# A transformer stack: compressed scores of the second token tile amid the first heads, the experts' choice ahead of the second tile's parts of X

## The chip, the cores and the metric

The kernel runs on one core of a Trainium2 chip. A core has TensorE (PE: matmuls, results in PSUM), VectorE (DVE), ScalarE (ACT), GpSimd (POOL) and SyncE (SP), each with its own queue, worked off in order; they wait for one another by semaphores. Transfers between HBM and on-chip memory are issued by SP and ACT. The metric is the device time of one execution in microseconds (us), as the median of several runs. TensorE's clock has two levels, 2.4 and 1.2 GHz; the profile gives the granted share (1.00 or 0.50).

## The reference: what is computed

256 tokens of 1024 numbers pass two blocks, and then a third of another kind, all in float32. Block one is windowed attention and a feed-forward. Block two, around which the change lies, is attention with three branches (compressed, selected and windowed keys) and a mixture of 8 experts, of which each token takes the best two:

```
s_c = einsum('bqkgd,bckd->bkgqc', qc, kcc) * scale          # compressed scores, 15 keys
p_c = _masked_softmax(s_c, cmp_end[None, :] <= tpos[:, None])
...
o = g[..., 0:1] * o_c + g[..., 1:2] * o_s + g[..., 2:3] * o_w
...
x = _layer_norm(DN_ALPHA * x + h, ln_gain[i, 0], ln_bias[i, 0])
...
logits = (xt @ router).astype(jnp.float32)
vals, ids = lax.top_k(logits, TOP_K)
w = jax.nn.softmax(vals, axis=-1)
gate = jnp.sum(jax.nn.one_hot(ids, N_EXPERTS) * w[..., None], axis=1)
for e in range(N_EXPERTS):
    out = out + gate[:, e:e + 1] * _swiglu(xt, w_gate[e], w_up[e], w_down[e])
```

Block three reads a memory of 256 further tokens, whose keys and values depend on no earlier block.

## The kernel before

Tokens stand in two tiles of 128 (`tt` 0 and 1). Each float32 weight tile is split into a high part (`wh`, a cast on ScalarE, L253 or L256) and a low part (`wl`, a subtraction on VectorE, L254 or L257), and a product is three matmuls (high by high, low by high, high by low: L274 to L276, and L1173 to L1175 in the experts). SP loads weights into a ring of raw tiles some tiles ahead. The order on each engine is set by a scheduler from the order in which the code is written, from priorities and from where pools of on-chip memory overlap: a pool that lies over another's place comes after it in that order.

The attention of block two (`nsa`) projects queries, keys and values, turns the queries of each tile (`rope64` on VectorE, transposes at L470, copies `qh`, `ql` at L474 and L475), and then computes compressed scores of both tiles, one after the other (L868 the mask, L872 24 matmuls of 32 columns a tile, L874 to L888 the softmax), in the two PSUM buffers of the pool `at`. Then come the heads, by `cc` and `tt`, in two halves each: scores in the four PSUM buffers of the pool `mm` (L909, mask L911), maximum (L913), exponentials on ScalarE (L917), transposes (L928), products with the values (L934 to L936) in an `at` buffer `ops`. Between the parts of the heads `fill` emits runs of the memory's keys and values of block three, L1900, which use `mm` as well and end with a copy `mkv` (L1903) and a store.

`route_load`, called when the heads are through in the code, loads the router's tables on ScalarE's queue (`rt` L964, `first` L976, `slots` L978, `uf` L981) into a pool `route`, and makes from them `gb` (the router times the norm's gain), `sums`, `c` (L973, L974) and `ub`.

`heads_out` multiplies by the output weights; `ln_part` adds and takes statistics, and for a tile that is complete calls `ln_rows`: transposes of the row that is not yet normed (L417, copied into `xT` at L418), mean and root (L382, L349, a power on POOL), and X in parts, `Xh` and `Xl`, by two passes on VectorE over 1024 columns, a cast on ScalarE and a subtraction (L424 to L428). These parts are what the experts gather their tokens from.

`moe` begins with the choice. Logits are the router's product with `xT` (L1002, 8 matmuls a tile, each two passes), corrected by mean and root (L1006 to L1008). Comparisons among the 8 logits, ties by `first`, give `sel` and `selb` (L1014 to L1022). Five small matmuls count places (L1025 to L1029), and `pos`, `cnt` and the one-hot tiles `oh` follow (L1031 to L1060). A branch on the count (L1131, L1132) comes before the first gather, matmuls of `oh` with `Xh` and `Xl` (L1106), and the experts' products.

Of the kernel before, what the change touches and what calls it, by code (L numbers as in the profile page):

```python
# [8 lines left out]
F32 = mybir.dt.float32  # L9
F32R = mybir.dt.float32r  # L10
BF16 = mybir.dt.bfloat16
AF = mybir.ActivationFunctionType
OP = mybir.AluOpType
# [3 lines left out]
P = 128  # L17
# [7 lines left out]
def f(ap):  # L25
    return ap.bitcast(F32)
# [72 lines left out]
class Net:  # L99
# [305 lines left out]
    def ln_rows(self, tt):  # L405


        nc, y = self.nc, self.y[tt]
        if not self.ln_xT:
            self.xT = self.xp.tile([P, KD, T], F32, tag="xh", name="xT")  # L410
            self.Xl = self.xp.tile([P, 2, D], F32R, tag="xl", name="Xl")
            self.Xh, self.lns, self.ln_xT = [], [], True
        hs = [slice(h * 512, h * 512 + 512) for h in range(2)]
        for h in range(2):
            tp = self.tr.tile([P, 4, P], F32, tag="tr", name="tr")
            for k in range(4):
                nc.tensor.transpose(tp[:, k], y[:, h * 512 + k * P:h * 512 + (k + 1) * P], self.idn)  # L417
            nc.scalar.copy(self.xT[:, h * 4:h * 4 + 4, tt * P:(tt + 1) * P], tp)  # L418
        mu, rs = self.ln_stats(tt)
        self.lns.append((mu, rs))  # L420
        Xh = self.xp.tile([P, D], F32R, tag=f"X{tt}", name="Xh")
        self.Xh.append(Xh)
        for s in hs:
            nc.vector.scalar_tensor_tensor(y[:, s], y[:, s], mu, self.lng[:, s], op0=OP.subtract, op1=OP.mult)  # L424
        for s in hs:
            nc.vector.scalar_tensor_tensor(y[:, s], y[:, s], rs, self.lnb[:, s], op0=OP.mult, op1=OP.add)
            nc.scalar.copy(Xh[:, s], y[:, s])
            nc.vector.tensor_sub(self.Xl[:, tt, s], y[:, s], f(Xh[:, s]))  # L428

    def ln_end(self):  # L430

# [273 lines left out]
    def nsa(self):  # L705
        nc, A, tc = self.nc, self.A, self.tc
        self.fine = True
        with ExitStack() as c0:
# [3 lines left out]
            p = c.enter_context(self.pool("nsa", 1))  # L712
# [148 lines left out]
            oh = po.tile([P, 8, T], F32R, tag="oh", name="oh")  # L861
            ol = po.tile([P, 8, T], F32R, tag="ol", name="ol")
            pc = []
            for tt in range(2):
                qs = slice(tt * P, (tt + 1) * P)
                e = ap.tile([P, 16, 16], F32, tag=f"ce{tt}", name="ce", bufs=1)
                sc = self.at.tile([P, 16, 16], F32, tag="at", name="at")
                nc.tensor.matmul(sc, self.idb, cmb[:, tt:tt + 1].to_broadcast([P, 16, 16]), start=True, stop=False)  # L868
                for i in range(8):
                    o = sc[:, 2 * i:2 * i + 2].rearrange("p h j -> p (h j)")  # L870
                    for n, (qn, kn) in enumerate(((0, 0), (0, 1), (1, 0))):
                        nc.tensor.matmul(o, qT[qn][:, i, qs], kcc[kn][:, i // 4].rearrange("p h j -> p (h j)"), start=False, stop=n == 2 and i == 7)  # L872
                dn = ap.tile([P, 16], F32, tag="cdn", name="cdn")
                nc.vector.tensor_reduce(dn, sc, axis=AX.X, op=OP.max)  # L874
                nc.vector.tensor_sub(e, sc, dn.unsqueeze(2).to_broadcast([P, 16, 16]))
                nc.scalar.activation(e, e, AF.Exp)
                nc.vector.tensor_reduce(dn, e, axis=AX.X, op=OP.add)
                nc.vector.tensor_scalar_max(dn, dn, 1e-30)
                nc.vector.reciprocal(dn, dn)
                dv = dn.rearrange("p (c g h) -> p c g h", c=2, h=2)  # L880
                for v in range(2):
                    nc.vector.tensor_mul(dv[:, v], dv[:, v], gate[tt][:, v * 8:v * 8 + 8, 0].rearrange("p (h g) -> p g h", h=2))
                nc.vector.tensor_mul(e, e, dn.unsqueeze(2).to_broadcast([P, 16, 16]))
                es = ap.tile([P, 8, 3, 32], F32R, tag=f"es{tt}", name="es", bufs=1)
                src = e.rearrange("p (i h) j -> p i (h j)", h=2)
                nc.scalar.copy(es[:, :, 0], src)
                nc.gpsimd.tensor_copy(es[:, :, 1], src)
                nc.vector.tensor_sub(es[:, :, 2], src, f(es[:, :, 0]))  # L888
                pc.append(es)
            for cc in range(2):  # L890
                for tt in range(2):
                    ops = self.at.tile([P, 512], F32, tag="at", name="ops")
                    nst = tt + 1
                    nh = 2 // nst
                    qs = slice(tt * P, (tt + 1) * P)
                    for half in range(2):
# [4 lines left out]
                        nm = ap.tile([P, 4, 2], F32, tag="nm", name="nm")  # L901
                        dn = ap.tile([P, 4, 2], F32, tag="dn", name="dn")
                        for b in range(4 // nh):
                            sc = self.mm.tile([P, nh, 2, nst, P], F32, tag="mm", name="sc")
# [19 lines left out]
                        for r, br in enumerate("sw"):  # L924
                            for st in range(nst):
# [9 lines left out]
                                nc.tensor.matmul(ops, vl, ph, start=False, stop=False)  # L935
                                nc.tensor.matmul(ops, vh, pl, start=False, stop=False)  # L936
                        self.fill(1 / 16, SOON)
                    tp = self.tr.tile([96, 4, P], F32, tag="tr", name="tr")
                    for g in range(4):
                        nc.tensor.transpose(tp[:, g], f(pc[tt][:, cc * 4 + g]).rearrange("p n j -> p (n j)"), self.idn)  # L940
# [17 lines left out]
    def route_load(self):  # L958

        nc, A, NE = self.nc, self.A, 8  # L960
        self.routes = ExitStack()
        p = self.routes.enter_context(self.pool("route", 1, side="right"))
# [19 lines left out]
        nc.vector.tensor_copy(ub[:, 0], uf)  # L982
        nc.vector.memset(ub[:, 1], 1.0)
        self.route = gb[:, 0], c, first, slots, ub, uf

    def moe(self):
        nc, A, tc = self.nc, self.A, self.tc
        self.first_block.close()
        Wg, Wu, Wd = A["moe_w_gate"][0], A["moe_w_up"][0], A["moe_w_down"][0]
        NE, F = 8, 3584  # L990
        NF = F // P
        with ExitStack() as c0:
# [2 lines left out]
            p2 = c0.enter_context(self.pool("moe2", 2))  # L995
            rt, lc, first, slots, ub, uf = self.route
            Xh, Xl = self.Xh, [self.Xl[:, tt] for tt in range(2)]
            L = p.tile([P, 2, NE], F32, name="L")
            for tt in range(2):
                lp = self.at.tile([P, NE], F32, tag="at", name="at")  # L1000
                for k in range(KD):
                    nc.tensor.matmul(lp, self.xT[:, k, tt * P:(tt + 1) * P], rt[:, k], start=k == 0, stop=k == KD - 1)  # L1002

                mu, rs = self.lns[tt]
                nm = p.tile([P, 1], F32, name=f"nm{tt}")
                nc.vector.tensor_scalar_mul(nm, mu, -1.0)  # L1006
                nc.vector.scalar_tensor_tensor(L[:, tt], lc[:, :NE], nm, lp, op0=OP.mult, op1=OP.add)
                nc.vector.scalar_tensor_tensor(L[:, tt], L[:, tt], rs, lc[:, NE:], op0=OP.mult, op1=OP.add)  # L1008

            b3 = [P, 2, NE, NE]  # L1010
            gt = p.tile(b3, F32, name="gt")
            eq = uf.rearrange("p (t a b) -> p t a b", t=2, a=NE)
            La, Lb = L.unsqueeze(2).to_broadcast(b3), L.unsqueeze(3).to_broadcast(b3)
            nc.vector.tensor_tensor(gt, La, Lb, op=OP.is_gt)  # L1014
            nc.vector.tensor_tensor(eq, La, Lb, op=OP.is_equal)
            nc.vector.tensor_mul(eq, eq, first.unsqueeze(1).to_broadcast(b3))
            nc.vector.tensor_add(gt, gt, eq)
            sel = p.tile([P, 2, NE], F32, name="sel")
            nc.vector.tensor_reduce(sel, gt, axis=AX.X, op=OP.add)
            selb = p.tile([P, 2, NE], BF16, name="selb")  # L1020
            nc.vector.tensor_single_scalar(selb, sel, 2.0, op=OP.is_lt)
            nc.vector.tensor_single_scalar(sel, sel, 2.0, op=OP.is_lt)  # L1022

            ps = self.at.tile([P, 3, NE], F32, tag="at", name="at")
            nc.tensor.matmul(ps[:, 0], ub[:, 0], selb[:, 0], start=True, stop=True)  # L1025
# [212 lines left out]
            for e in range(NE):  # L1238
# [4 lines left out]
                hs = []  # L1243
# [905 lines left out]
```

## Time and profile before

| | us |
|---|---|
| median of 3 runs | 2332.0 |
| the runs | 2325.09, 2332.0, 2341.94 |
| the profiled execution | 2328.03 |
| its span, first to last instruction | 2326.2 |
| TensorE busy in the span | 2229.0 (96%) |
| VectorE busy | 1799.7 (77%) |
| ScalarE busy | 1477.1 (63%) |

A page of the profile gives busy time by engine, the chain of work that ended last and the costliest groups of instructions; timelines give each instruction with the idle time of its engine before it and what ended it. A matmul's busy time is modelled and includes overlap with the next one, so matmuls are read by their starts. Attention of block two, from its compressed scores on, lies from 434 to about 560 us; the output projection from there to 578; the choice from 578 to 591; the experts from 591.

### The profile page before, as it was taken

How to read it: one execution, taken by the hardware profiler on the slowest of the kernel's cores; microseconds unless marked ns; L12 is line 12 of the kernel's file. 1: busy time of each engine (PE TensorE's matmuls, PEld its weight loads, DVE VectorE, ACT ScalarE, POOL GpSimd, SP SyncE). 2: the span in 40 equal slices, each digit the busy share in tenths (PEclk: the TensorE clock that was granted, in tenths of full speed). 3: DMA queues.
4: the chain of work that ended last, by engine and by line, in shares of the span. 5: the costliest groups of instructions: out<-in, count | busy, mean ns of one | idle time of the engine just before them, and what ended most of it. 6: DMA issues, size and time to landing. Idle time of an engine off the chain costs nothing.

```text
span 2326.2 us, 35748 instructions
## 1 busy us (share of the span) xinstructions
PE 2229.0 (96%) x12969; PEld 1930.2 (83%) x12969; DVE 1799.7 (77%) x2854; ACT 1477.1 (63%) x2390; POOL 66.8 (3%) x78
## 2 busy tenths in 40 slices
PE   8999998999899999999999999996999899999998
PEld 6699987878788888888888888885889888988997
DVE  7765558766899999999999999997866855666664
ACT  5654436575687778787878777874553554455553
POOL 0000000000000000000000000001110110000000
PEclk9999999999899999999999999998999999999999
DMA  8366655434999999999999999984323323544751
GB/s 246 96 203 190 192 167 172 156 103 142 318 372 369 342 354 370 366 373 329 364 373 369 341 358 370 368 300 117 109 73 101 94 62 107 162 154 165 229 195 46
DMA packets 319708, 541.92 MB, mean 233 GB/s; under 512 B 21839, under 2 KB 95015, under 8 KB 319271
## 3 DMA queue, kind: packets, MB, share of 16 engines
q1 hardware_dynamic: 309680, 528.93, 66.7%
q10 hardware_dynamic: 9847, 10.67, 1.5%
q8 instruction: 103, 1.69, 0.3%
q14 instruction: 78, 0.64, 0.1%
HBM read 536.38 MB, written 3.15 MB: 232 GB/s over the span
## 4 chain that ended last, share of the span: by engine, by line
PE 87%; DVE 6%; issue 3%; ACT 2%; DMA 1%; POOL 1%; SPq 0%; DVEq 0%; POOLq 0%; ACTq 0%
PE mm L1173 13%; PE mm L1175 13%; PE mm L1174 13%; PE mm L276 5%; PE mm L274 5%; PE mm L275 5%; PE mm L691 3%; PE mm L690 3%; PE mm L689 3%; PE mm L1900 2%; PE mm L318 1%; PE mm L319 1%; PE mm L317 1%; DVE wl L254 1%; PE sc L909 1%
## 5 line engine op out<-in xcount | busy, mean ns | idle before, releaser
L257 DVE TENSOR_TENSOR wl<-w,wh 128x1024 fp32r<-128x1024 f32 x755 | 905.9, 1222 | 182.3 <-ACT wh L256 155.1
L256 ACT CAST wh<-w 128x1024 fp32r<-128x1024 f32 x755 | 788.3, 1053 | 298.7 <-PE mm L1175 166.9
L1173 PE MATMUL mm<-wh,xg 128*128 128x512 f32 x896 | 354.1, 395 | 0.0
L1175 PE MATMUL mm<-wh,xg 128*128 128x512 f32 x896 | 349.6, 390 | 0.0
L1174 PE MATMUL mm<-wl,xg 128*128 128x512 f32 x896 | 349.2, 390 | 0.0
L253 ACT CAST wh<-w 128x512 fp32r<-128x512 f32 (+1 forms) x362 | 207.3, 615 | 125.4 <-PE mm L276 56.1
L254 DVE TENSOR_TENSOR wl<-w,wh 128x512 fp32r<-128x512 f32 (+1 forms) x362 | 237.1, 682 | 42.4 <-ACT wh L253 40.4
L1175 PEld LDWEIGHTS mm<-wh,xg 128*128 128x128 f32 x896 | 168.4, 188 | 35.9
L1174 PEld LDWEIGHTS mm<-wl,xg 128*128 128x128 f32 x896 | 168.6, 188 | 33.5
L1173 PEld LDWEIGHTS mm<-wh,xg 128*128 128x128 f32 x896 | 168.5, 188 | 33.4 <-DVE xg L1111 0.2
L689 PE MATMUL mm<-xh,wh 128*128 128x256 f32 x672 | 187.2, 279 | 0.0
L690 PE MATMUL mm<-xh,wl 128*128 128x256 f32 x672 | 187.1, 278 | 0.0
L691 PE MATMUL mm<-xl,wh 128*128 128x256 f32 x672 | 187.1, 278 | 0.0
L1174 PE MATMUL mm<-wl,h 128*128 128x512 f32 x448 | 175.2, 391 | 0.0
L1173 PE MATMUL mm<-wh,h 128*128 128x512 f32 x448 | 174.9, 390 | 0.0
L1175 PE MATMUL mm<-wh,h 128*128 128x512 f32 x448 | 174.5, 389 | 0.0
L689 PEld LDWEIGHTS mm<-xh,wh 128*128 128x128 f32 x672 | 127.4, 190 | 0.0
L690 PEld LDWEIGHTS mm<-xh,wl 128*128 128x128 f32 x672 | 126.1, 188 | 0.0
L691 PEld LDWEIGHTS mm<-xl,wh 128*128 128x128 f32 x672 | 126.2, 188 | 0.0
L248 DVE SCALAR_TENSOR_TENSOR wl<-w,cols,wh 128x512 fp32r<-128x512 f32 (+1 forms) x128 | 77.7, 649 | 47.2 <-ACT wh L247 47.1
L247 ACT ACTIVATE wh<-w,cols 128x512 fp32r<-128x512 f32 (+1 forms) x128 | 74.6, 635 | 45.1 <-issue 23.2
L1175 PEld LDWEIGHTS mm<-wh,h 128*128 128x128 f32 x448 | 84.1, 188 | 18.0 <-issue 0.5
(620 smaller groups left out, 4494.1 us busy)
## 6 DMA issues: line engine op xcount, KB each, us to landing
w<-in_moe_w_gate_dram SPq DMA_DIRECT2D x224, 512.0 KB, 5.5
w<-in_moe_w_up_dram SPq DMA_DIRECT2D x224, 512.0 KB, 5.6
w<-in_moe_w_down_dram SPq DMA_DIRECT2D x216, 512.0 KB, 5.8
w<-in_w_in_dram SPq DMA_DIRECT2D x60, 512.0 KB, 3.9
w<-in_w_ffn_in_dram SPq DMA_DIRECT2D x40, 512.0 KB, 9.8
w<-in_ffn_w_gate_dram SPq DMA_DIRECT2D x28, 512.0 KB, 4.4
w<-in_ffn_w_up_dram SPq DMA_DIRECT2D x28, 512.0 KB, 4.4
w<-in_ffn_w_down_dram SPq DMA_DIRECT2D x28, 512.0 KB, 3.6
```

Source lines behind the costliest of these rows:

```text
L253: nc.scalar.copy(wh[:, ks, :n], w[:, ks, :n])
L254: nc.vector.tensor_sub(wl[:, ks, :n], w[:, ks, :n], f(wh[:, ks, :n]))
L256: nc.scalar.copy(wh[:, :nk, :n], w[:, :nk, :n])
L257: nc.vector.tensor_sub(wl[:, :nk, :n], w[:, :nk, :n], f(wh[:, :nk, :n]))
L274: nc.tensor.matmul(o, h, wh[:, k, :sn], start=k0 + k == 0, stop=False)
L275: nc.tensor.matmul(o, h, wl[:, k, :sn], start=False, stop=False)
L689: nc.tensor.matmul(o, wh[:, k, js], h, start=first and j % 2 == 0, stop=False)
L690: nc.tensor.matmul(o, wl[:, k, js], h, start=False, stop=False)
L691: nc.tensor.matmul(o, wh[:, k, js], l, start=False, stop=last and j % 2 == 1)
L1173: nc.tensor.matmul(ps, h, wh[:, k], start=k0 + k == 0, stop=False)
L1174: nc.tensor.matmul(ps, h, wl[:, k], start=False, stop=False)
L1175: nc.tensor.matmul(ps, l, wh[:, k], start=False, stop=k0 + k == nk - 1)
```

## The change

The compressed scores become a function `compressed(tt)`. It is called for the first tile ahead of the first head, after the head's `ops` buffer is taken, and for the second tile after the first half of that head. Its PSUM tile comes from `mm` instead of `at`. In `ln_rows` the second tile's parts of X are put off: `moe` emits them after `selb`, and `issue_after` orders each of them behind `selb` on its engine. The choice's small tiles (`L`, `nm`, `gt`, `sel`, `selb`) move from the pool `moe` to `route`, 832 bytes a partition more there.

```diff
@@ ln_rows
-        for s in hs:
-            nc.vector.scalar_tensor_tensor(y[:, s], y[:, s], mu, self.lng[:, s], op0=OP.subtract, op1=OP.mult)
-        for s in hs:
-            nc.vector.scalar_tensor_tensor(y[:, s], y[:, s], rs, self.lnb[:, s], op0=OP.mult, op1=OP.add)
-            nc.scalar.copy(Xh[:, s], y[:, s])
-            nc.vector.tensor_sub(self.Xl[:, tt, s], y[:, s], f(Xh[:, s]))
+        def parts(ins=None):
+            with self.tc.issue_after(ins) if ins else ExitStack():
+                for s in hs:
+                    nc.vector.scalar_tensor_tensor(y[:, s], y[:, s], mu, self.lng[:, s], op0=OP.subtract, op1=OP.mult)
+                for s in hs:
+                    nc.vector.scalar_tensor_tensor(y[:, s], y[:, s], rs, self.lnb[:, s], op0=OP.mult, op1=OP.add)
+                    nc.scalar.copy(Xh[:, s], y[:, s])
+                    nc.vector.tensor_sub(self.Xl[:, tt, s], y[:, s], f(Xh[:, s]))
+        if tt:
+            self.rest = parts
+        else:
+            parts()
@@ nsa
-            for tt in range(2):
+            def compressed(tt):
...
-                sc = self.at.tile([P, 16, 16], F32, tag="at", name="at")
+                sc = self.mm.tile([P, 16, 16], F32, tag="mm", name="sc")
...
                     ops = self.at.tile([P, 512], F32, tag="at", name="ops")
+                    if cc == 0 and tt == 0:
+                        compressed(0)
...
                         self.fill(1 / 16, SOON)
+                        if cc == 0 and tt == 0 and half == 0:
+                            compressed(1)
@@ route_load
+        self.rp = p
@@ moe
-            L = p.tile([P, 2, NE], F32, name="L")
+            rp = self.rp
+            L = rp.tile([P, 2, NE], F32, name="L")
...
-            nc.vector.tensor_single_scalar(selb, sel, 2.0, op=OP.is_lt)
+            chosen = nc.vector.tensor_single_scalar(selb, sel, 2.0, op=OP.is_lt)
             nc.vector.tensor_single_scalar(sel, sel, 2.0, op=OP.is_lt)
+            self.rest(chosen.ins)
```

Three places of the built programs' order follow. Line numbers of the change are 9 to 17 higher than before for the same statement (L964 is now L978, L1002 is now L1018).

ScalarE, the loads of the router's tables, before: amid the casts of the first compression weights.

```order
L824 COPY two<-mm 128x512
L253 CAST wh<-w 128x2x256
L964 DMA rt<-in_moe_router_dram 128x8x8
L253 CAST wh<-w 128x2x256
L976 DMA first<-in_first_dram 128x64
L978 DMA slots<-in_slots_dram 128x128
L981 DMA uf<-in_before_dram 128x128
```

The same loads in the changed program: at the block's end, behind the copy of `xT` and the last `mkv`.

```order
L418 COPY xT<-tr 128x4x128
L1920 COPY mkv<-mm 128x512
L978 DMA rt<-in_moe_router_dram 128x8x8
L990 DMA first<-in_first_dram 128x64
L992 DMA slots<-in_slots_dram 128x128
L995 DMA uf<-in_before_dram 128x128
L430 CAST Xh<-y_5804 128x512 x2
```

What moved are the four loads, past the whole attention and the output projection. In the built programs the pool `route` begins at byte 148,672 of a partition before and at 147,840 now, both times up to 151,424; the attention's pool, which holds `mkv`, ends at 148,160 in both.

VectorE after the second tile's statistics (`rs`), before: parts of X (L424 to L428), then logits and choice.

```order
L349 TENSOR_SCALAR rs<-mv 128x1
L424 SCALAR_TENSOR_TENSOR y_5804<-y_5804,mv,lng 128x512 x2
L426 SCALAR_TENSOR_TENSOR y_5804<-y_5804,rs,lnb 128x512 x2
L428 TENSOR_TENSOR Xl<-y_5804,Xh 128x512
L1006 TENSOR_SCALAR nm_6062<-mv 128x1
L428 TENSOR_TENSOR Xl<-y_5804,Xh 128x512
L1007 SCALAR_TENSOR_TENSOR L<-c,nm_6062,at 128x8
```

The changed program from the same `rs`, and further on from `selb`.

```order
L349 TENSOR_SCALAR rs<-mv 128x1
L985 MEMSET one 128x1
L997 MEMSET ub 128x128
L1022 TENSOR_SCALAR nm_6054<-mv 128x1
L1022 TENSOR_SCALAR nm_6067<-mv 128x1
L982 TENSOR_TENSOR gb<-rt,cols 128x64 x2
L984 TENSOR_REDUCE sums<-gb 128x16
L988 COPY c<-at 128x16
L1023 SCALAR_TENSOR_TENSOR L<-c,nm_6054,at 128x8
```

```order
L1037 TENSOR_SCALAR selb<-sel 128x16
L427 SCALAR_TENSOR_TENSOR y_5804<-y_5804,mv,lng 128x512
L1038 TENSOR_SCALAR sel<-sel 128x16
L427 SCALAR_TENSOR_TENSOR y_5804<-y_5804,mv,lng 128x512
L429 SCALAR_TENSOR_TENSOR y_5804<-y_5804,rs,lnb 128x512 x2
L431 TENSOR_TENSOR Xl<-y_5804,Xh 128x512
L1048 COPY pos<-at 128x16
L431 TENSOR_TENSOR Xl<-y_5804,Xh 128x512
```

The parts moved behind `selb`, and `gb`, `sums` and `c`, which stood before the heads or among them, moved to the place between `rs` and the logits.

TensorE there, and in the changed program: the router's matmuls (`at<-gb,xT`), once before and once now.

```order
L417 MATMUL tr<-idn,y_5804 128x128 x4
L1002 MATMUL at<-gb,xT 128x8 x8
L417 MATMUL tr<-idn,y_5804 128x128 x4
L1002 MATMUL at<-gb,xT 128x8 x8
L1025 LDWEIGHTS ub
```

```order
L417 MATMUL tr<-idn,y_5804 128x128 x8
L987 MATMUL at<-sums,one 128x16
L1018 MATMUL at<-gb,xT 128x8 x16
L1042 LDWEIGHTS ub
```

The matmul for `c` moved from amid the last heads to just ahead of the router's, which now all stand behind the transposes. In the attention, TensorE's queue before has 12 compressed matmuls of each tile one after the other; in the changed program, 12 of the first tile, 12 score matmuls of the first head with the queries' transposes (L479) among them, the other 12, then 30 of the memory's with the second tile's transposes among them, and then all 24 of the second tile.

## Rows read from the trace of the kernel before

**Rows 1.** The page, part 1: busy us (share of the span) xinstructions, by engine.
```profile
PE 2229.0 (96%) x12969; PEld 1930.2 (83%) x12969; DVE 1799.7 (77%) x2854; ACT 1477.1 (63%) x2390; POOL 66.8 (3%) x78
```
**Rows 2.** Busy time by stretch: length, engines' busy (x), granted clock, DMA share, GB/s.
```profile
585.00:590.00 5.00, 0.28 (x5) 0.19 (x4) 4.72 (x27) 1.89 (x4) 0.00 (x0) 0.50 0.99 367
590.00:595.00 5.00, 3.73 (x17) 3.76 (x18) 2.02 (x6) 1.87 (x2) 0.00 (x0) 0.50 0.47 172
```
**Rows 3.** Timeline of TensorE: start, us, engine, line, what [idle before <-releaser].
```profile
578.47 1.85 PE L1002 MATMUL at<-gb,xT 128*128 128x8 f32 x16
...
580.65 2.08 PE L1002 MATMUL at<-gb,xT 128*128 128x8 f32 x16
588.68 0.17 PE L1025 MATMUL at<-selb,ub 128*128 128x8 bf16 x1 [5.95 <-DVE selb L1021]
...
591.27 1.20 PE L1106 MATMUL mm<-oh,Xh 128*128 128x256 f32 x4 [2.30 <-DVE cnt L1133]
```
**Rows 4.** Timeline of VectorE in the same stretch.
```profile
582.03 1.40 DVE L424 SCALAR_TENSOR_TENSOR y<-y,mv,lng 128x512 f32<-128x512 f32 x2
583.36 1.40 DVE L426 SCALAR_TENSOR_TENSOR y<-y,rs,lnb 128x512 f32<-128x512 f32 x2
584.78 0.69 DVE L428 TENSOR_TENSOR Xl<-y,Xh 128x512 fp32r<-128x512 f32 x1
...
585.46 0.68 DVE L428 TENSOR_TENSOR Xl<-y,Xh 128x512 fp32r<-128x512 f32 x1
...
586.45 0.22 DVE L1007 SCALAR_TENSOR_TENSOR L<-c,nm,at 128x8 f32<-128x8 f32 x1
...
588.46 0.17 DVE L1021 TENSOR_SCALAR selb<-sel 128x16 bf16<-128x16 f32 x1
```
**Rows 5.** Timeline of ScalarE: the last copy of the memory's keys and values.
```profile
581.33 0.59 ACT L1903 COPY mkv<-mm 128x512 f32<-128x512 f32 x1
```
**Rows 6.** The tile `rt`: its load, at 368.9, and the time to landing.
```profile
L964 ACTq DMA_DIRECT2D rt<-in_moe_router_dram x1: 381/381/381, 368.9 to 368.9; - x1
...
DMA to landing us min/median/max: 2.4/2.4/2.4
```
**Rows 7.** Timeline of SyncE's queue, at the choice.
```profile
583.06 1.13 SPq L220 DMA_DIRECT2D parked<-in_moe_w_down_dram  x2
```
**Rows 8.** Transfers from 540 to 625: count, KB each, median us to landing.
```profile
parked<-in_moe_w_down_dram SPq DMA_DIRECT2D x4, 1024.0 KB, 6.5
```
**Rows 9.** Timeline of VectorE where the tables are made ready.
```profile
374.75 0.35 DVE L968 TENSOR_TENSOR gb<-rt,cols 128x64 f32<-128x64 f32 x2
...
375.16 0.40 DVE L970 TENSOR_REDUCE sums<-gb 128x16 f32<-128x128 f32 x1
```
**Rows 10.** Line 973: its matmul, ns min/median/max, first and last start.
```profile
L973 PE MATMUL at<-sums,one x2: 179/220/262, 529.1 to 529.1; 128*128 128x16 f32 x2
```
**Rows 11.** Timeline of TensorE: compressed scores at full and at half clock.
```profile
434.12 0.26 PE L872 MATMUL at<-kch,qh 128*128 128x32 f32 x1
434.23 0.26 PE L872 MATMUL at<-kcl,qh 128*128 128x32 f32 x1
...
442.05 0.38 PE L872 MATMUL at<-kcl,qh 128*128 128x32 f32 x1
442.26 0.37 PE L872 MATMUL at<-kch,ql 128*128 128x32 f32 x1
```
**Rows 12.** Timeline of ScalarE behind the tables' loads.
```profile
373.48 0.62 ACT L253 CAST wh<-w 128x512 fp32r<-128x512 f32 x1 [2.07 <-DMA first<-in_first_dram]
```
**Rows 13.** Busy time by stretch, attention.
```profile
439.00:449.00 10.00, 10.00 (x42) 8.89 (x41) 3.98 (x9) 1.23 (x2) 0.00 (x0) 0.50 0.18 57
```
**Rows 14.** Timeline of ScalarE, the block's first exponential.
```profile
447.75 0.59 ACT L474 CAST qh<-tr 128x512 fp32r<-128x512 f32 x1 [9.01 <-PE tr L470]
...
449.65 0.37 ACT L917 ACTIVATE pn<-sc,nm 128x128 f32<-128x128 f32 x1
```
**Rows 15.** Line 872: who waited for it (us, times).
```profile
  DVE cdn L874: 4.1, 2
```

More of the change, by code (lines that the diff above doesn't have):

```diff
@@ L1004, in moe @@
                 mu, rs = self.lns[tt]
-                nm = p.tile([P, 1], F32, name=f"nm{tt}")
+                nm = rp.tile([P, 1], F32, name=f"nm{tt}")
                 nc.vector.tensor_scalar_mul(nm, mu, -1.0)
@@ L1010, in moe @@
             b3 = [P, 2, NE, NE]
-            gt = p.tile(b3, F32, name="gt")
+            gt = rp.tile(b3, F32, name="gt")
             eq = uf.rearrange("p (t a b) -> p t a b", t=2, a=NE)
@@ L1017, in moe @@
             nc.vector.tensor_add(gt, gt, eq)
-            sel = p.tile([P, 2, NE], F32, name="sel")
+            sel = rp.tile([P, 2, NE], F32, name="sel")
             nc.vector.tensor_reduce(sel, gt, axis=AX.X, op=OP.add)
-            selb = p.tile([P, 2, NE], BF16, name="selb")
-            nc.vector.tensor_single_scalar(selb, sel, 2.0, op=OP.is_lt)
+            selb = rp.tile([P, 2, NE], BF16, name="selb")
+            chosen = nc.vector.tensor_single_scalar(selb, sel, 2.0, op=OP.is_lt)
             nc.vector.tensor_single_scalar(sel, sel, 2.0, op=OP.is_lt)
+            self.rest(chosen.ins)
             ps = self.at.tile([P, 3, NE], F32, tag="at", name="at")
```

## Prediction

> **What bounds the kernel now.** I read the page first, then a table of stretches around the two places that the change touches, then each engine's timeline there, then the queue of transfers. The page has TensorE busy 96% of the span [rows 1], so work that is moved on another engine counts only where TensorE waits for it. The second place of the change, the step from the second attention block into the experts, is such a place: between 585 and 590 us TensorE is busy 0.28 of 5 us, and its granted clock is 0.50, the lower of its two levels; from 590 to 595 it is still 0.50 [rows 2]. TensorE's own timeline says who ends the gap: the router's 32 small matmuls (two groups of 16) are over by 582.73, then it sits idle 5.95 us for VectorE's `selb`, then 2.30 us more before the first gather of the experts at 591.27 [rows 3]. VectorE in that gap is nearly never idle: the second token tile's parts of X (1.40 + 1.40 + 0.69 + 0.68 = 4.17 us) run first, then the logits, then the choice, with `selb` starting at 588.46 [rows 4]. So this gap is bound by VectorE's sum of work. The order of that work alone gives little back, since the gather needs the parts and the choice both.
>
> **Part 1: the choice ahead of the parts.** The order of the changed program shows more than the diff says. The four loads of the router's tables stood on ScalarE's queue near the start of the block; now they stand behind the last copy of the memory's keys and values. Nothing of the choice can run before them: `gb` is the router matmuls' operand, `c` and `first` enter the logits and ties, `uf` the counting. Step by step, from one execution:
>
> - Issue: that copy starts at 581.33 and takes 0.59 [rows 5], so the load of `rt` is issued no earlier than 581.92.
> - Landing: with little else in flight it took 2.4 us [rows 6], which gives 584.3 as the lower end. Here SyncE has just issued two transfers of 1 MB, at 583.06, behind weight tiles, and transfers of that load take 6.5 us to land (median) [rows 7, 8]; the DMA share is 0.99 from 585 to 590 [rows 2]. The nearest row is that one, since it is in the same stretch; `rt` is smaller, so I take 6.0 and have it land at 588.0. Upper end: behind everything queued up to 584.2 plus 6.5, 590.7.
> - `gb` twice 0.35, `sums` 0.40 [rows 9], then the two passes of the matmul for `c`, some 0.3 [rows 10]: 1.1 us to 589.1.
> - The 32 router passes took 1.85 + 2.08 = 3.93 us at full clock [rows 3]. Now TensorE has been idle since before them. Its small matmuls of the compressed scores follow each other in 0.11 us at full clock (434.12 to 434.23) and in 0.21 us at half (442.05 to 442.26) [rows 11]. The clock is at half from before 585 on [rows 2], so I take 3.93 x 0.21/0.11 = 7.5 us; ends 3.9 and 7.9. They end at 596.6.
> - From the second tile's first logit step (586.45) to `selb` (588.46) 2.0 us [rows 4]: `selb` at 598.6, 10.1 us later than before.
> - From `selb` to the gather was 591.27 - 588.46 = 2.8 us [rows 3, 4]. The four parts, 4.17 us [rows 4], now stand in that piece on VectorE, since they are ordered behind `selb`; the gather starts at 598.6 + 2.8 + 4.2 = 605.6, that is 14.3 us later.
>
> The lower end of the terms (584.3 + 1.1 + 3.9 + 2.0 = 591.3, plus 7.0) is 598.3, or +7.0; the upper (590.7 + 1.1 + 7.9 + 2.0 + 7.0 = 608.7) is +17.4. The cost is not hidden: TensorE has no other work there, as the 5.95 us show [rows 3]. Behind the waiting `gb` on VectorE stand only the logits, the choice and the parts; on ScalarE, behind the loads, only the two copies of X's high part. SyncE's next weights wait for the same branch as the gather and move with it. Had the tables been there in time, the gain would be what VectorE idles between `selb` and the one-hots, under 1 us.
>
> The Trainium skill, "DMA: Bandwidth & Descriptors", section "Queues, rings and completion order", speaks against a small load that is issued late beside big ones: each DMA engine takes turns between queues, and drains some 9 to 17 descriptors of one before it turns to the next. The router's table is 1024 runs of 32 bytes, 64 for each of 16 engines, so 4 to 7 turns; with runs of 2 KB at 367 GB/s (0.09 us each) in the other queue, a turn of that queue would be 0.8 to 1.5 us, and 4 to 7 of them about 6 us on top of the 2.4, an estimate by that page of 590.1 for the landing. By it the sum would be 2.1 us larger. No row here shows the turns, so the sum stays with 588.0.
>
> Where the loads stood before, a copy of weights on ScalarE waited 2.07 us behind them [rows 12]. TensorE does not stop in that stretch, so I cost its removal at nothing; if the weights were the limit there, up to 2 us would come back, which the range covers.
>
> **Part 2: compressed scores of the second token tile later.** The same 48 matmuls of both tiles run; nothing is added. Before, 24 of them stood at once behind the last projection, and from 439 to 449 us the clock was at 0.50 [rows 13]. ScalarE's first exponential of the block came at 449.65, behind the copy of the second tile's queries at 447.75, which had waited 9.01 us for TensorE's transposes [rows 14]. Now scores of the first head stand between the two pieces, the transposes come ahead of the second tile's compressed scores, and these stand behind 30 of the memory's matmuls. Best end: the whole 10 us run at full speed, 10 x 0.5 = 5.0 us of TensorE's work back, and TensorE is the bound here. Other end: the clock falls all the same, and as the scores now take one of four accumulator buffers that the heads use too, the wait of VectorE for compressed scores (4.1 us in two waits [rows 15]) turns up once more in the heads: +4.1. Nothing tells how the clock will fall with the mixed order; fewer small matmuls in a row speak for some gain. I take half of the best end, -2.5.
>
> **Sum.** 14.3 - 2.5 = +11.8 us. On the profiled execution, 2328.0, that is 2339.8. The median of the three runs is 2332.0, 4.0 higher, so for a median 2343.8; I say 2343.
>
> **The rivals.**
>
> 1. *Forecast, the tables come late*: +11.8; with its ends +2.0 (7.0 - 5.0) to +21.5 (17.4 + 4.1), mostly 2335 to 2352. For it: the order, and the busy queues [rows 2, 8]. Chance 0.60.
> 2. *Faster: the attention gives back more than the tables cost.* Place: 434 to 450 us. If the half-speed stretch goes (5.0) and the chain of exponentials, which now starts 5 us sooner, sets the end of the block as well, the gain is 10; with the tables at their low end of +7.0 the time is 2332 - 3 = 2329. It decides where the attention gains over 7.0. Against it: the memory's matmuls fill TensorE there, so an earlier chain and a faster clock are hardly both worth their whole. Chance 0.14.
> 3. *The tables land nearly in time*: 2.4 us as in the quiet stretch, and the router matmuls at full clock: +7.0 - 2.5 = +4.5, 2336.5. Against it: DMA share 0.99 [rows 2]. Chance 0.13.
> 4. *Slower still: buffers.* The heads wait for accumulators, +4.1, and the tables cost their upper end: 2332 + 21.5 = 2353.5. For it: four buffers now serve the projections' ends, both compressed scores, the heads' scores and the memory's runs. Chance 0.13.
>
> **How the numbers follow.** The forecast's time is 2343. The range leaves out the outer halves of rivals 2 and 4 and the rare sum of several ends: 2328 to 2354. One per cent, 23 us, is what a measurement of this kernel can tell from no change, as single runs spread over 17 us. Under 2309 there is no case worked out: 0.03. Over 2355 only rival 4 with the skill's slower landing and a slow run: 0.08. Within: 0.89.
>
> **What would show it.** Late loads: ScalarE's issue of `rt` near 582 instead of 369, landing near 588. VectorE: idle after the second `rs` until `gb`, `selb` near 598.6, the parts behind it. TensorE: 32 router passes between 589 and 597 at 0.21 us each, then idle once more, the gather near 605. In the attention: first exponential near 445 to 447, a shorter stretch at 0.50. I am wrong if `rt` lands before 585, if the router passes run at full clock, or if the block's last attention matmul moves by more than 5 us either way.

## The result

The changed kernel takes 2355.48 us (median of 7 runs, 2349.36 to 2366.48), the kernel before 2337.43 (7 runs, 2325.09 to 2344.49); the ratio is 1.0087, 95% interval 1.0066 to 1.0108. Forecast were 2343 and a range of 2328 to 2354. It is slower, as forecast, but by 18 us between the medians (20 by the ratio) instead of 12, and 1.5 us above the range. The forecast counted from 2332.0, the median of the first 3 runs of the kernel before; over 7 runs that median is 5.4 us higher.

Where the 26.2 us between the two profiled executions (spans 2326.2 and 2352.4) lie was read by taking each instruction of VectorE and ScalarE that stands in both traces, and its start in the one less its start in the other. The median of that offset grows in steps (places are times of the kernel before):

```
stretch, us        change of the offset, us
0 to 150           -0.3
150 to 290         +3.9   both programs are the same here (see the first experiment)
290 to 430         +1.5
430 to 495         -2.6   attention: the moved scores
495 to 570         -0.2
570 to 610        +13.4   from the block's last matmul to the experts
610 to 1530        +8.1   the experts, evenly over the whole stage
1530 to the end    +2.3
```

The two sizes that the prediction worked out, -2.5 and +14.3, are nearly there (-2.6 and +13.4). The 8.1 us of the experts were not in it.

### The profile page after: what moved, and what is told of

Read it like the earlier page. It is cut to its first block, busy times and chain, and to the rows that moved or that the text cites. A ratio compares the mean times of both kernels' runs of the same rounds, so it can differ in the third digit from the quotient of the medians.

```text
span 2352.4 us, 35746 instructions
## 1 busy us (share of the span) xinstructions
PE 2245.6 (95%) x12969; PEld 1942.7 (83%) x12969; DVE 1802.7 (77%) x2854; ACT 1475.6 (63%) x2390; POOL 65.8 (3%) x78
## 4 chain that ended last, share of the span: by engine, by line
PE 88%; DVE 5%; issue 3%; ACT 2%; DMA 1%; POOL 1%; SPq 0%; DVEq 0%; POOLq 0%; ACTq 0%
PE mm L1190 13%; PE mm L1192 13%; PE mm L1191 13%; PE mm L274 5%; PE mm L276 5%; PE mm L275 5%; PE mm L699 3%; PE mm L698 3%; PE mm L700 3%; PE mm L1917 2%; PE mm L318 1%; PE mm L319 1%; PE mm L317 1%; PE tr L1222 1%; PE sc L921 1%
## 5 line engine op out<-in xcount | busy, mean ns | idle before, releaser
L1190 PE MATMUL mm<-wh,xg 128*128 128x512 f32 x896 | 357.3, 399 | 0.0
L1190 PEld LDWEIGHTS mm<-wh,xg 128*128 128x128 f32 x896 | 168.8, 188 | 32.8 <-DVE xg L1128 0.2
L699 PE MATMUL mm<-xh,wl 128*128 128x256 f32 x672 | 188.6, 281 | 0.0
L1190 PE MATMUL mm<-wh,h 128*128 128x512 f32 x448 | 176.8, 395 | 0.0
L699 PEld LDWEIGHTS mm<-xh,wl 128*128 128x128 f32 x672 | 126.2, 188 | 0.0
```

The lines of the kernel that those rows point to most:

```text
L699: nc.tensor.matmul(o, wl[:, k, js], h, start=False, stop=False)
L1190: nc.tensor.matmul(ps, h, wh[:, k], start=k0 + k == 0, stop=False)
```

## The profile after

Part 1 of the page, as [rows 1]:

```profile
PE 2245.6 (95%) x12969; PEld 1942.7 (83%) x12969; DVE 1802.7 (77%) x2854; ACT 1475.6 (63%) x2390; POOL 65.8 (3%) x78
```

TensorE has the same 12,969 matmuls and is busy 16.6 us longer: more than idle time was added. The stretches at the choice, as [rows 2] (length, engines' busy (x), granted clock, DMA share, GB/s):

```profile
585.00:590.00 5.00, 0.62 (x3) 0.63 (x4) 0.74 (x3) 0.00 (x0) 0.04 (x1) 0.50 0.94 281
...
600.00:605.00 5.00, 0.00 (x0) 0.00 (x0) 4.92 (x18) 2.76 (x6) 0.00 (x0) 0.50 0.82 315
605.00:610.00 5.00, 3.61 (x17) 3.64 (x18) 1.52 (x4) 1.74 (x2) 0.00 (x0) 0.50 0.60 203
```

One gap of TensorE has become two: one in which VectorE is idle as well and waits for the table `rt`, and one in which VectorE does the parts. TensorE's timeline there, against [rows 3]:

```profile
582.02 0.63 PE L417 MATMUL tr<-idn,y 128*128 128x128 f32 x4 [1.10 <-ACT xT L418]
589.38 0.61 PE L987 MATMUL at<-sums,one 128*128 128x16 f32 x2 [6.72 <-DVE sums L984]
589.83 6.97 PE L1018 MATMUL at<-gb,xT 128*128 128x8 f32 x32
599.15 0.17 PE L1042 MATMUL at<-selb,ub 128*128 128x8 bf16 x1 [2.36 <-DVE selb L1037]
...
606.39 1.19 PE L1123 MATMUL mm<-oh,Xh 128*128 128x256 f32 x4 [6.96 <-DVE cnt L1150]
```

The 32 router passes stand behind the table, at half clock: 6.97 us instead of 3.93. VectorE, against [rows 4] (L427 to L431 are L424 to L428 of before):

```profile
588.55 0.36 DVE L982 TENSOR_TENSOR gb<-rt,cols 128x64 f32<-128x64 f32 x2 [3.91 <-DMA rt<-in_moe_router_dram]
588.94 0.38 DVE L984 TENSOR_REDUCE sums<-gb 128x16 f32<-128x128 f32 x1
...
596.84 0.22 DVE L1023 SCALAR_TENSOR_TENSOR L<-c,nm,at 128x8 f32<-128x8 f32 x1 [2.79 <-PE at L1018]
...
598.92 0.17 DVE L1037 TENSOR_SCALAR selb<-sel 128x16 bf16<-128x16 f32 x1
599.01 0.74 DVE L427 SCALAR_TENSOR_TENSOR y<-y,mv,lng 128x512 f32<-128x512 f32 x1
...
602.53 0.68 DVE L431 TENSOR_TENSOR Xl<-y,Xh 128x512 fp32r<-128x512 f32 x1
```

The tile `rt`, as [rows 6]: issued at 582.7, landed 5.8 us later.

```profile
L978 ACTq DMA_DIRECT2D rt<-in_moe_router_dram x1: 386/386/386, 582.7 to 582.7; - x1
...
DMA to landing us min/median/max: 5.8/5.8/5.8
```

In the attention, as [rows 13] and [rows 14], the stretch at half clock is shorter, and the first exponential comes at 451.41, which is 446.3 on the clock of before (the offset there is 5.1), 3.3 earlier:

```profile
439.00:444.00 5.00, 5.00 (x35) 3.92 (x33) 3.30 (x8) 1.73 (x3) 0.00 (x0) 1.00 0.94 303
444.00:449.00 5.00, 4.67 (x25) 4.57 (x25) 3.27 (x7) 0.00 (x0) 0.00 (x0) 0.60 0.35 115
449.00:454.00 5.00, 5.00 (x35) 4.96 (x33) 2.47 (x6) 4.46 (x16) 0.00 (x0) 0.72 0.01 2
```

```profile
449.51 0.59 ACT L483 CAST qh<-tr 128x512 fp32r<-128x512 f32 x1 [5.84 <-PE tr L479]
...
451.41 0.37 ACT L929 ACTIVATE pn<-sc,nm 128x128 f32<-128x128 f32 x1
```

The wait of VectorE for compressed scores is 2.6 us in one, where [rows 15] had 4.1 in two; the accumulators that rival 4 feared are not waited for. TensorE's own waits from 434 to 560 (us, times, longest) are these two, both for an operand:

```profile
PE sc L882 <- DVE ql L484: 0.3, 1, 0.3
PE tr L940 <- DVE pn L935: 0.2, 1, 0.2
```

The experts. 800 us in the midst of that stage, first before, then after (columns as in [rows 2]):

```profile
700.00:1500.00 800.00, 797.23 (x3659) 660.79 (x3658) 742.77 (x711) 630.08 (x666) 0.00 (x0) 1.00 1.00 360
```
```profile
700.00:1500.00 800.00, 797.31 (x3624) 655.51 (x3623) 736.69 (x702) 623.52 (x657) 0.00 (x0) 1.00 0.99 357
```

TensorE is as busy, at the same granted clock of 1.00, and gets through 3624 matmuls instead of 3659. That is 1% fewer, as the offset grows by some 7 us in that stretch. The median distance between the starts of two of its matmuls rises from 227 to 229 ns: 232 up to the second of a group of three (L1190), 226 up to the third, 229 to the next group. Nothing is waited for; the matmuls themselves go slower. What differs: the six tiles that left the pool `moe` (`L`, the two `nm`, `gt`, `sel`, `selb`: 832 bytes in each partition) stood ahead of the gathered tokens `xg` and the hidden `h`, so these lie 832 bytes lower. `xg` began at byte 57,216 of a partition and now begins at 56,384; the weights are where they were (`wh` from 151,424, `wl` from 171,904, both 128 past a multiple of 256).

A matmul has an operand that is held (loaded by a weight load, PEld; 128*128 in the rows) and one that is streamed past it. In the experts the gathered tokens or the hidden values are held, and 512 columns of weights are streamed; in L689 it is the other way round, 128 columns of weights are held and the 256 tokens of `xh` streamed:

```
nc.tensor.matmul(ps, h, wh[:, k], ...)        # L1173: h is xg or the hidden h, wh[:, k] has 512 columns
...
nc.tensor.matmul(o, wh[:, k, js], h, ...)     # L689: wh[:, k, js] has 128 columns, h is xh
```

Some of the expectations below name the two operands of the experts the other way round (`xg` moving, the weights stationary). The distance between their places, on which the argument rests, is the same either way.

## The experiments

All were timed in five rounds against the kernel before; ratios carry their 95% interval, over all the runs of a kernel. Last come the offsets of all profiled executions, one execution of each kernel, in one table.

**The same kernel again.** No edit.

> The changed kernel once more, unchanged, to see which part of the 26.2 us between the two profiled executions comes back. In that pair 3.9 us came at 170 to 265 us, where both programs are the same, -2.6 in the attention, 13.4 between the block's last matmul and the first gather, and 8.7 over the whole expert stage, where TensorE's median distance between matmuls was 229 instead of 227 ns. Theory A, the late tables alone cost time and the slower pace is an accident of that execution: pace of 227 ns, ratio 1.005 (12.8 less 2.6 of 2337 is 1.004 to 1.006). Rival B, the slower pace belongs to the changed program: 229 ns again, ratio 1.008 to 1.010.

Measured: 1.0073 (1.0047 to 1.0099). The experts' 8.1 us come back to a tenth, the attention's -2.8 and the gap's 12.3 too; the 3.9 us at 150 to 290 don't. So the slow pace is the program's (rival B), and the 3.9 us are one execution's. The median of this second set of runs is 2348.76, inside the forecast's range, 14.4 above that of the kernel before beside it (2334.41): that the first one lay outside is in part chance, the 8.1 us are not.

The 3.9 us lie in the 1,152 matmuls of L689 to L691 (256 columns of `xh`) between 136 and 271 us, at the same addresses in both programs. From the first start to the last they take 134.5 us in some executions (before, this one, and three below) and 138.4 in others (after, and five below): 113 or 118 ns from start to start, one or the other for a whole stretch. The counts from 185 to 255, before and after:

```profile
185.00:255.00 70.00, 70.00 (x620) 70.00 (x620) 40.27 (x40) 34.07 (x40) 0.00 (x0) 1.00 0.66 195
```
```profile
185.00:255.00 70.00, 70.00 (x596) 70.00 (x596) 38.62 (x39) 33.01 (x40) 0.00 (x0) 1.00 0.64 188
```

This execution has 620 there, like before. What chooses between the two is not known.

**Tables early.** The comparison's result is written over the scaled router weights. That takes 512 bytes from the pool `route`, which then begins at 148,352 and no longer overlaps the attention's pool (up to 148,160), and the loads go back to 377 us.

```
-        self.rp = p
+        self.rp, self.gb2 = p, gb
...
-            gt = rp.tile(b3, F32, name="gt")
+            gt = self.gb2
```

> The changed kernel with one tile less in the pool route (the comparison's result is written over the router's scaled weights, which are dead by then), so that the pool no longer overlaps the memory's tiles and the tables are loaded at the start of the block again. Choice still ahead of the parts, scores still moved. Theory A: the tables' lateness is the whole cost, so router matmuls run near 582 at full clock, selb near 585, the gather within 1.5 us of its place before (591.3 less what the attention gives back), ratio 0.997 to 1.000. Rival B, the pace in the expert stage comes with the new addresses: gather as in A, but 229 ns and ratio 1.002 to 1.004. Rival C, the parts between choice and gather are what cost: gather 4 us later than in A, ratio 1.001 to 1.002.

Measured: 1.0032 (1.0011 to 1.0054). The gap costs 1.2 us instead of 12 to 13, so the lateness was nearly the whole of it. The experts' 8.1 us stay: rival B.

**Moved scores alone.** Before, with `compressed` as in the change.

> Before with the compressed scores moved and nothing else; tables early, parts ahead of the choice. Theory A: the attention gives back 2.6 us as in the changed kernel (block's last matmul 2 to 3 us earlier than in before, measured from the block's projections), all later offsets stay there, ratio 0.998 to 1.000. Rival, the accumulators shared with the heads cost as much as the clock gives: 1.000 to 1.002.

Measured: 0.9975 (0.9951 to 0.9999). The attention gives 2.8 us by 495 us; 1.6 go again at 520 us, where this execution has 3.4 us at half clock; and the experts run at the old pace. Theory A. The same dip of the clock between 515 and 535 is in the runs with a loss of 1.2 to 1.6 in that column, one without the moved scores among them, and in none of those near 0. A part of the ratio, 6.9 us in the third block, is not the scores': 3.8 of it are 864 matmuls of L689 to L691 at 113 instead of 118 ns (99.2 us against 103.0), which the run without the moved scores has as well; the rest stays open.

**Choice alone.** The change without the moved scores.

> The change without the moved scores: tables late, choice ahead of the parts. Theory A: gather some 15 us later than before (13.4 plus the 2.6 that the attention does not give back is 13 to 16), ratio 1.006. Rival B, the pace of the expert stage comes with the late tables or the new addresses: 229 ns, ratio 1.009 to 1.011.

Measured: 1.0086 (1.0058 to 1.0114). No gain in the attention (0.0), gap 12.9, experts 7.9: rival B again, and by stretches the two parts of the change add up.

**The changed kernel with `xg` and `h` 64 bytes higher.** An unused tile at the head of `moe` sets where the others lie. Every engine's order of instructions stays that of the changed kernel.

```
-            p.tile([P, 48], F32, name="lead")
+            p.tile([P, 64], F32, name="lead")
```

> The changed kernel with the unused tile at the head of the pool moe 64 bytes longer, which puts the gathered tokens xg and the hidden h back on multiples of 128 bytes (in the changed kernel they start 64 past one). Theory A, the start of the matmuls' moving operand sets the pace: 227 ns instead of 229 in the expert stage, its drift of 8.1 to 8.7 us gone, the late tables' 12 to 13 us stay, ratio 1.004 to 1.005. Rival B, the slower pace comes with something else that the choice or its pool brought: 229 ns, ratio 1.007 to 1.009.

Measured: 1.0051 (1.0028 to 1.0073). The 8.1 us are gone, to 0.0, and TensorE is back at before's count:

```profile
700.00:1500.00 800.00, 797.23 (x3657) 660.71 (x3657) 742.85 (x709) 629.91 (x664) 0.00 (x0) 1.00 1.00 360
```

The gap's 12.4 us stay, and not one instruction changed its place. Where the tiles lie is thus the cause of the pace, and nothing of the choice.

**The same 64 bytes in the kernel before,** and nothing else; the same edit, and every engine's order that of before.

> Before with the same 64 bytes added and nothing else, so that xg and h start 64 bytes past a multiple of 128. Theory A: TensorE's median distance in the expert stage rises from 227 to 229 ns (232 for the first of three matmuls, 229 for the third, 226 for the second), 8.1 to 8.7 us over the stage, no jump before it, ratio 1.0035. Rival B: 227 ns, ratio 1.000.

Measured: 1.0102 (1.0068 to 1.0135), nearly three times what was expected. The offset jumps nowhere at the choice (0.2) and grows by 22.7 us over the experts:

```profile
700.00:1500.00 800.00, 797.49 (x3569) 645.14 (x3568) 727.56 (x692) 612.96 (x647) 0.00 (x0) 1.00 0.98 352
```

The median distance is 233 ns here, with `xg` at 57,280. So the place has more than a good and a bad value.

**Both repairs:** tables early, and `xg` and `h` 64 bytes higher.

> The changed kernel with both repairs: tables early (one tile less in route), xg and h on multiples of 128. Theory A: pace 227 ns, gather within 1.5 us of before's, the attention's 2.7 us kept: ratio 0.9975 to 0.999, like the moved scores alone (0.9975). Rival, the choice ahead of the parts costs something by itself: 1.000 to 1.002.

Measured: 0.9977 (0.9953 to 1.0002), with no difference from the moved scores alone that can be measured. Gap and experts cost 1.3 and 0.0. TensorE's timeline at the choice:

```profile
584.88 1.85 PE L1018 MATMUL at<-gb,xT 128*128 128x8 f32 x16
...
587.06 1.90 PE L1018 MATMUL at<-gb,xT 128*128 128x8 f32 x16
591.76 0.17 PE L1042 MATMUL at<-selb,ub 128*128 128x8 bf16 x1 [2.80 <-DVE selb L1037]
...
599.00 1.19 PE L1123 MATMUL mm<-oh,Xh 128*128 128x256 f32 x4 [6.97 <-DVE cnt L1150]
```

With the offset of 6.4 us taken off, `selb`'s matmuls come at 585.4 instead of 588.68 [rows 3], and the gather at 592.6 instead of 591.27. The choice is 3 us earlier and the gather 1 us later: it waits for the parts, which moved behind the choice. VectorE does them from 591.61 to 595.81, ahead of the counting:

```profile
591.61 0.74 DVE L427 SCALAR_TENSOR_TENSOR y<-y,mv,lng 128x512 f32<-128x512 f32 x1
...
595.13 0.68 DVE L431 TENSOR_TENSOR Xl<-y,Xh 128x512 fp32r<-128x512 f32 x1
```

The choice's new order gains nothing even with the tables in time.

**All operands at even places.** Both repairs, and 64 bytes at the head of the long-lived pool `xp`, with the alignment tiles of the pools behind it taken out.

```
+        self.xp.tile([P, 16], F32, name="lead")
...
-            po.tile([P, 16], F32, name="lead")
```

> The version with both repairs, and 64 bytes more at the head of the kernel's long-lived pool xp (the alignment tiles behind it taken out, so that the rest stays even): xh, xl, Xh, Xl, and the mixers' operands, until now 64 past a multiple of 128, start on one. By theory A the matmuls that stream xh (624 of 512 columns at 229 to 232 ns, 864 of 256 at 117 to 118) go at 227 and 113 to 114: 624 x 3.3 ns = 2 us, and up to 864 x 4.4 ns = 3.8 us where TensorE doesn't wait otherwise; 2 to 6 us faster than the version with both repairs, ratio 0.995 to 0.998. Rival B: the same as that version.

Measured: 1.0047 (1.0022 to 1.0073), slower than both repairs alone, so the expectation failed. The experts keep their pace, but the matmuls of L697 to L699 (L689 to L691 in before, `xh` streamed past held weights) get slower, at 185 to 255 us 586 in 70 us where before had 620 and after 596:

```profile
185.00:255.00 70.00, 70.00 (x586) 70.00 (x585) 37.29 (x38) 32.47 (x38) 0.00 (x0) 1.00 0.60 182
```

Their median distance is 120 ns in both stretches of them, against 113 in the first and 118 in the last of before. "Even is fast" is no rule.

**Another odd place in before:** `lead` 64 bytes shorter, `xg` at 57,152.

```
-            p.tile([P, 48], F32, name="lead")
+            p.tile([P, 32], F32, name="lead")
```

> Before with the unused tile at the head of the pool moe 64 bytes shorter instead of longer: xg and h again start 64 bytes past a multiple of 128, at another place (320 past a multiple of 512; 448 in the run with 64 bytes more, 64 in the changed kernel). Theory A, any odd multiple of 64 slows the 512-column matmuls, the amount by the place: 229 to 233 ns instead of 227, 8 to 24 us, ratio 1.0035 to 1.010. Rival B, only some places do: 227 ns, ratio 1.000.

Measured: 1.0043 (1.0019 to 1.0066); 8.1 us over the experts and the 226, 229 and 232 ns of the changed kernel, with not one instruction moved. Theory A, at the price of the changed kernel:

```profile
700.00:1500.00 800.00, 797.32 (x3625) 655.53 (x3625) 736.79 (x704) 623.76 (x659) 0.00 (x0) 1.00 0.99 357
```

**Both repairs, and everything from `xp` on 128 bytes higher.**

```
+        self.xp.tile([P, 32], F32, name="lead")
```

> The version with both repairs, everything from the long-lived pool xp on moved by 128 bytes, so that odd multiples of 64 stay odd and even ones even. Theory A, odd or even is what counts: 227 ns in the expert stage, ratio within 0.002 of the version with both repairs (0.9977). Rival B, the place within 512 bytes counts as well: other paces, 113 to 118 ns for the 256-column matmuls on xh become another value, as the 120 ns of the all-even version; 1.000 or more.

Measured: 1.0126 (1.0091 to 1.0161). `xg` begins on a multiple of 256 now and the experts lose 21.4 us, at 231 to 232 ns. So theory A, odd or even, falls; the place within 256 bytes counts.

```profile
700.00:1500.00 800.00, 797.49 (x3574) 646.20 (x3573) 728.84 (x693) 613.84 (x647) 0.00 (x0) 1.00 0.98 352
```

**Parts first, tables late.** The changed kernel with `xg` 64 bytes higher, and the parts not held back:

```
-        if tt:
-            self.rest = parts
-        else:
-            parts()
+        parts()
...
-            self.rest(chosen.ins)
```

> The changed kernel with xg and h on multiples of 128 and the second tile's parts ahead of the choice again, as in before; the tables still late. Against the same kernel with the parts behind the choice (1.0051). Theory A: the 4.2 us of parts now run while VectorE waits for the router's table, so selb stays at its place and the gather comes 4 us earlier: 8 to 9 us later than before instead of 12.3, ratio 1.003. Rival, the parts delay something on the choice's path, and the gather comes no earlier: 1.005.

Measured: 1.0073 (1.0041 to 1.0105), and the gap costs 15.8 us, not 8 to 9: the expectation failed, and on a path that neither theory had. The casts of the parts (`Xh`, on ScalarE) now stand ahead of the loads in ScalarE's queue:

```profile
590.67 1.28 ACT L430 CAST Xh<-y 128x512 fp32r<-128x512 f32 x2 [2.48 <-DVE y L429]
592.71 0.39 ACTq L975 DMA_DIRECT2D rt<-in_moe_router_dram  x1
```

That is 586.2 on the clock of before, where the changed kernel issued at 580.4; and SyncE had begun to issue its transfers of 1 MB at 589.59, ahead of the load, which took 8.4 us instead of 5.8 to 6.3.

```profile
DMA to landing us min/median/max: 8.4/8.4/8.4
```

With the tables late, the change's order of the choice is the better one by this trace (12.4 against 15.8 us); the intervals of the two ratios overlap.

**The weights moved instead.** Before, with the tile at the right edge of SBUF 64 bytes longer: the weights begin at 151,360, `xg` stays, and no instruction moves.

```
-EDGE = 24
+EDGE = 40
```

> Before with the tile at the right edge of SBUF 64 bytes longer, so that the weights' tiles (wh, wl, w, the stationary operand of the experts' matmuls) start 320 instead of 384 past a multiple of 512, and xg and h stay where they are in before (384). Every engine's order is that of before. So far, by xg's place past a multiple of 256 with the weights at 128: 128 gave 227 ns, 64 gave 229, 192 and 0 gave 232 to 233. Theory A, the streamed operand's own place counts: 227 ns in the expert stage, no drift there. Rival B, the distance between the two operands' places counts: now it is 64, as in the run with xg at 448, so about 233 ns, some 24 us over the stage, ratio 1.010. The 256-column matmuls that stream weights and hold xh may change pace under either.

Measured: 1.0177 (1.0132 to 1.0221). Rival B: 233 ns, 22.6 us over the experts, as in the run with the same distance (22.7). The count for 700 to 1500:

```profile
700.00:1500.00 800.00, 797.48 (x3571) 644.40 (x3570) 727.67 (x692) 613.53 (x647) 0.00 (x0) 1.00 0.98 352
```

So the place of `xg` alone doesn't set the pace, nor, by the runs that moved `xg`, that of the weights alone. The 256-column matmuls of L689 to L691 went to 120 ns with it, as in the run with all at even places: the two runs come to distance 0 by moving either operand, and their 1,152 matmuls take 141.6 us in both. This speaks for the distance. Not shown for the 512-column ones is a run with both operands moved by 64; without it, it isn't excluded that each has a best place of its own. What else the ratio has beyond the experts was not taken apart.

The growth of the offset against before, in us, by the stretches of the first table (the distance is `xg`'s start less the weights', as a remainder within 256 bytes):

```
run                 distance  0-150  -290  -430  attn  -570   gap  experts  rest
after                    -64   -0.3   3.9   1.5  -2.6  -0.2  13.4      8.1   2.3
the same again           -64   -1.0   0.0   2.6  -2.8   1.3  12.3      8.1  -1.0
tables early             -64    7.7   0.0   0.2  -4.3   0.1   1.2      8.1  -2.2
scores alone               0   -0.8   3.9   2.1  -2.8   1.6   0.6      0.0  -6.9
choice alone             -64   10.4   0.0   0.4   0.0   1.3  12.9      7.9   1.5
after, 64 higher           0   -0.8   3.9   2.3  -2.8   1.2  12.4      0.0  -1.3
before, 64 higher        +64    7.5   3.9   1.5   1.4  -0.1   0.2     22.7   1.2
both repairs               0    1.8   3.9   2.2  -2.9   1.4   1.3      0.0  -0.2
all even                   0   -0.3   6.1   1.2  -1.1   0.3   1.7      0.2   9.1
before, 64 lower         -64    1.4   3.9   1.2   0.0   0.0   0.4      8.1   2.1
both, 128 higher         128    1.6   4.6   5.6  -1.0   0.3   2.0     21.4   1.5
parts first                0    7.8   0.0   0.3  -2.9   1.3  15.8      0.1   3.3
weights 64 lower         +64   11.2   6.7   4.5   1.8   2.0   0.7     22.6  15.0
```

The experts' column agrees within 0.2 us by distance, whatever else a kernel does. The first and the last column scatter by 11 us and more between executions; so do the times. The second is the pace of L689 to L691: 0.0 where their stretch takes 134.5 us, 3.9 where it takes 138.4, more in the three kernels in which the distance of their own operands differs.

## Why the prediction was wrong

- **Tables late, right.** It was read from the order, and the terms held. Issue: 582.70, which is 580.4 on before's clock, 1.5 earlier than I had it, since the load went out before the copy ahead of it had begun (583.37). Landing: 5.8 us, where I took 6.0 from transfers of 1 MB; these came only at 596.8, though, and the transfers in flight were weight tiles of 512 KB, so that the size came out right is in part luck. The estimate by the Trainium skill, "DMA: Bandwidth & Descriptors", section "Queues, rings and completion order", came to 8.2 us. The changed kernel's 5.8 speak against it, the 8.4 of the run with parts first, beside 1 MB transfers, would fit; no trace shows the turns. Tables made ready: 589.83 - 588.55 = 1.3 (1.1). Router passes: 6.97 (7.5, scaled from 3.93, whose last pass stood at half clock already; wholly at full clock they took 3.75 in the version with both repairs). Last logits to `selb`: 2.08 (2.0). `selb` to the gather: 7.47 (7.0). Sum: the gather at 606.39, less the offset of 2.3 us at the block's end 604.1, which is 12.8 later than before, where 14.3 was forecast; 12.3 to 13.4 by the executions.
- **Attention, right in sign and size, its cause in part.** -2.6 to -2.9 us by 495 in six of seven executions with the moved scores (those with `xp` moved, -1.0 and -1.1, left aside), -4.3 in the seventh, for a forecast of -2.5; first exponential at 446.3 (445 to 447 forecast). The forecast took it all from the clock; the stretch at 0.50 shrank from 10 us to some 6.8 (5 x 2 x 0.40 and 5 x 2 x 0.28 in the rows above), which at half speed is 1.6 us. Where the other 1 us comes from was not taken apart.
- **The choice's order, wrong in sign, and small.** "Under 1 us" to be gained with the tables in time; the runs show 0.5 to 1.1 us lost (gap of 1.2 and 1.3, against 0.2 to 0.7 with the old order).
- **The sum, wrong.** The step that failed: "14.3 - 2.5 = +11.8" takes the gather's delay for the whole kernel's. It has the experts' stage move rigidly behind the gather ("SyncE's next weights wait for the same branch as the gather and move with it"), with no term and no bound for its own pace, since it held the same instructions in the same order. I followed the tiles that move from the pool `moe` to the pool `route` only for what they do to the order of the loads. But every tile behind those in `moe` moved by 832 bytes, and 4,032 matmuls of 512 columns, 2.0 ns longer each, made 8.1 us of it. With the terms as measured, 12.8 - 2.6 + 8.1 = 18.3 us; the medians differ by 18.1. So of the 12.5 us between 2343 and 2355.48, 6.5 are these terms (18.3 instead of 11.8), and 5.4 the base, which rose from 2332.0 to 2337.43 with more runs. That part is chance.
- **Rival 4** named a time that came close, 2353.5, by a mechanism that didn't occur. Its accumulators are not waited for, and the gap did not reach its upper end; that its time lies near is luck.

Not settled: which part of the chip makes the place count, why the 256-column matmuls prefer another distance than the 512-column ones, and why those on `xh` go at 113 ns in one stretch and at 118 in another, with the same places.

## What to carry to other kernels

A tile that changes pools moves all that lies behind it in the old pool. So compare the addresses of the large operands before and after a change, as one compares the order, and where the place differs give the stage that multiplies them a term of its own, however little its code changed. A pool that grows by less than a kilobyte can delay loads by 200 us of program, where it comes to overlap a pool that lives longer: here 320 bytes moved the loads from 369 to 583 us.

## What the runs showed of the hardware

- The pace of back-to-back float32 matmuls depends on where the two operands begin in their partition. By the held operand's start less the streamed one's, as a remainder within 256 bytes: with 512 columns of weights streamed past held tokens, 0 gave 227 ns from start to start; -64, 226 to 232 (median 229); +64, 233; 128, 231 to 232. With 256 columns of `xh` streamed past held weights: +64 (before), 113 or 118, one of them for a whole stretch of an execution; -64 (everything 128 higher), 118; 0, 120. Of the distances measured, the best for the one is the worst for the other. The granted clock was 1.00 in these stretches, so it doesn't tell of this.
- A 32 KB load issued amid weight tiles took 5.8 to 6.3 us to land in four executions and 8.4 in one, against 2.4 to 2.5 in a quiet stretch.
- TensorE at half clock took 6.97 us for the 32 small router passes that took 3.75 at full clock in the version with both repairs (1.85 + 1.90).
